# Two decoder layers on one core: key norms in four token quarters, three main passes behind each small product, pooling's products one gate strip later

## The chip, the core and the metric

The kernel runs on one core of a Trainium2 chip. TensorE multiplies, VectorE (DVE) and ScalarE (ACT) do the elementwise work, GpSimd (POOL) a little of it, and the queues of SyncE (SP) and ScalarE issue transfers. The metric is the device time of one execution in microseconds (us), lower is better.

## What is computed

Two layers are applied to 288 tokens: 256 of a prompt and 8 groups of 4 sample tokens. Each layer is a SwiGLU feed-forward block, a mixer, and a second feed-forward block. The mixer adds an RWKV-7 recurrence and a causal pooling, each behind a sigmoid gate. What matters here, cut from the reference:

```python
kk = hs((k * k_k).astype(f32))                       # 8 heads of 64
kk = kk / jnp.maximum(jnp.sqrt(jnp.sum(kk * kk, axis=-1, keepdims=True)), 1e-12)
k = hs(k.astype(f32) * (1 + (a - 1) * k_a.astype(f32)))
S_T, y = lax.scan(_wkv_step, wkv0, (r, decay, k, v, -kk, kk * a))   # over the tokens
d = pooled - pb                                      # windows of 2, 4, 8, 16 tokens
y = jnp.einsum('blgc,gcd->blgd', d, w_pool)
merged = gates[..., :D_MODEL] * (ya @ w_br_a) + gates[..., D_MODEL:] * (yb @ w_br_b)
x = x + mod[:, :, 5] * (merged @ w_out)
```

`kk` is the removal key: it is divided by its norm over each head, for each token.

## The kernel before, in words

Activations lie with features on the 128 partitions and the 288 tokens along the free axis. Weights arrive in slots of eight 128x128 tiles (`raw`, three buffers). Every four tiles ScalarE writes the rounded part `wh` (L225) and VectorE the remainder `wl` (L226); `mm3` then makes three matmuls of each tile (L251), chained in one fixed order. These are the main passes.

The mixer has two streams for TensorE. The first are its main passes, yielded by `main_ops` two tiles at a time, so a step is six main matmuls. There are 136 steps in a layer: 22 strips of four steps (`MAIN`: the input projections "in" 5 to 14; gates "ga" 8 and 9; pooling's four input strips "in" 15 to 18, each followed by one of the gate strips 10 to 13; gate strips 14 and 15), eight strips "bb" of two steps, and eight gate strips 0 to 7 of four steps. After them come the strips "ba", which read the recurrence's result, and then "wo".

The second stream is the recurrence: small fp32 products with ScalarE and VectorE work between them. Its order in the code is: `lora_mm` and the squared keys; norms (`kps`, `rn`) and running decay sums; scaled keys `AR` and `BK`, for which `head_spread` copies a row per head onto 64 partitions; four `scores`; a triangular elimination on VectorE (L945, L947); products that invert blocks; then a loop over four chunks of 64 tokens with state `S`; `outputs(0)` and `outputs(1)` with a group norm; transposes, and `split` into `yah` and `yal`, which "ba" reads. Beside it run the sample tokens' products: `smp_state` four times, and `smp_last` four times, each of which loads a 256 KB state into one shared buffer and writes it back.

The two streams are merged by hand. `fill()` takes its next count from `PLAN` and pops that many items of a queue; with an empty queue an item is one main step. `add` puts a small product on the queue, and `WEAVE` main steps behind it. `need(99)` runs all main steps that are left. A planner then orders the instructions of each engine by this order as priority and by its own durations, and may pull main passes forward where it expects TensorE to be free.

Pooling: `pooled(g)` runs on VectorE after strip "in" 15+g and writes `dd` (two buffers); `pool_out(g)` multiplies it (L706) after a gate strip, and writes `ybh`, `ybl`, which "bb" reads.

The norms before: for each pair of heads `j`, four matmuls put the sums of squares of 288 tokens into rows 32j and 32j+1 of `kps`; a square root, a maximum and a reciprocal run over 128 x 288; `head_spread` reads 32 rows for each pair.

Of the kernel before, what the change touches and what calls it, by code (L numbers as in the profile page):

```python
# [20 lines left out]
AF = mybir.ActivationFunctionType  # L21
# [4 lines left out]
P = 128  # L26
D = 1024
KD = 8
# [7 lines left out]
HP = 4  # L36
# [29 lines left out]
TOK = (0, P, NT - P)  # L66
SLOT = 8
PRIO = 75
WEAVE = 2
PLAN = (1, 0, 0, 11, 1, 15, 12, 16, 5, 6, 2, 0, 10, 12, 2, 2, 1, 8, 13, 1, 2, 8, 4, 2, 3, 0, 5, 1, 1, 7)  # L70
FIRST = 3
RMS = {0: 0.25, 1: 0.15, 2: 0.25}
SPREAD = {0: 0.45, 1: 0.4, 2: 0.45}
# [63 lines left out]
for _n, _w in PARAMS:  # L137
# [1 line left out]
    _o += _w  # L139
NPAR = _o  # L140

CONSTS = [("ones", 1), ("eps", 1), ("ident", 128), ("mhalf", 1), ("hs", 32), ("hb", 128),
          ("maskp", 128), ("masks", 64), ("bmask", 8), ("id32", 32), ("id16", 16), ("halves", 2), ("scan", 288),
          ("rc", 64)]
COFF, _o = {}, 0
# [6 lines left out]
def make_consts():  # L152
    c = np.zeros((P, NCST), np.float32)

    def put(name, a):
        o, w = COFF[name]
        c[: a.shape[0], o:o + w] = a.reshape(a.shape[0], w)

    p = np.arange(P)
    put("ident", np.eye(P, dtype=np.float32))  # L160
    put("mhalf", np.full((P, 1), -0.5, np.float32))
    put("ones", np.ones((P, 1), np.float32))
    hs = np.zeros((P, 32), np.float32)
    hb = np.zeros((P, P), np.float32)
    for e in range(2):
        hs[64 * e:64 * e + 64, e] = 1.0
        hb[e::32, 64 * e:64 * e + 64] = 1.0
    put("hs", hs)
    put("hb", hb)
    s, t = p % 64, np.arange(64)  # L170
    put("maskp", np.stack([s[:, None] < t, s[:, None] <= t], 1).astype(np.float32))
    s, t = p % 32, np.arange(32)
    blk = s[:, None] // TS == t // TS
    put("masks", np.stack([blk & (s[:, None] < t), blk & (s[:, None] <= t)], 1).astype(np.float32))
    put("bmask", ((p % 32)[:, None] // TS == np.arange(NB)).astype(np.float32))
    put("id32", ((p % 32)[:, None] == np.arange(32)).astype(np.float32))
    put("id16", ((p % 16)[:, None] == np.arange(16)).astype(np.float32))
    put("halves", (p % 32 // 16)[:, None] == np.arange(2))
    sc = np.ones(NT, np.float32)
    sc[0:TP:CH] = 0.0  # L180
    sc[TP::TS] = 0.0
    put("scan", np.broadcast_to(sc, (P, NT)))
    rc = np.stack([1.0 / np.minimum(w, np.arange(16) + 1) for w in WINDOWS]).astype(np.float32)
    put("rc", np.broadcast_to(rc, (P, 4, 16)))
    put("eps", np.full((P, 1), NORM_EPS, np.float32))
    return c


class Kernel:
# [433 lines left out]
    def mixer(self, l):  # L623
# [13 lines left out]
        def tj(name):  # L637
# [17 lines left out]
        V.tensor_tensor(out=shs, in0=shs, in1=self.par(l, "mu").unsqueeze(2).to_broadcast([P, NPA, NB]), op=ALU.mult)  # L655
        V.tensor_scalar(mu1, self.par(l, "mu"), -1.0, 1.0, op0=ALU.mult, op1=ALU.add)
        rks = tl([P, HP, 32], "rks")
        G.tensor_tensor(out=rks, in0=self.cst("hs").unsqueeze(1).to_broadcast([P, HP, 32]),
                        in1=self.par(l, "r_k").unsqueeze(2).to_broadcast([P, HP, 32]), op=ALU.mult)
        V.tensor_scalar(ka1, self.par(l, "k_a"), -1.0, 1.0, op0=ALU.mult, op1=ALU.add)  # L660
        ident, hs, hb = self.cst("ident"), self.cst("hs"), self.cst("hb")

        def shifted(i, ps, dst):

# [78 lines left out]
        def main_ops():  # L743

            for n, (name, m) in enumerate(MAIN):
                pre = name == "in" and m < PRE_M
                for ps in strip(name, m, xh=self.vh, xl=self.vl, w=NV) if pre else strip(name, m):
                    yield n
                if (name, m) == ("in", PRE_M - 1):
                    self.v_cm.__exit__(None, None, None)  # L750
                with tc.high_priority(offset=PRIO):
                    if pre:
                        project_pre(m, ps)
                    elif name == "in":
                        project(m, ps)
                    else:
                        S.activation(out=t2s[0][:, m - KD, :], in_=ps[:, :NT], func=AF.Sigmoid,
                                     bias=self.par(l, "b_gate", m))
                if name == "in" and m == 14:
                    nc.sync.dma_start(out=self.io["o_shift"][l], in_=sho)  # L760
                if name == "in" and m == 14:
                    t2s.append(tl([P, KD, NT], "t2"))
                if name == "ga":
                    if m - KD - 2 in dds:
                        pool_out(m - KD - 2, dds[m - KD - 2])
                    self.mod_step()
            at_bb = len(MAIN)
            for m in range(KD):
# [47 lines left out]

        def head_spread(rows, j):
            ps = self.ps_wk()
            T.matmul(ps[:, :NT], hb[32 * j:32 * j + 32, :], rows[32 * j:32 * j + 32, :], start=True, stop=True)
            return ps[:, :NT]  # L820

        halves = [slice(0, 64), slice(64, 128)]
# [8 lines left out]
        for j in range(HP):  # L831
            lora_mm(j)
            t = tl([P, NT], "tj", "kk2", bufs=3)
            S.activation(out=t, in_=xk[:, j, :], func=AF.Square, scale=self.par(l, "k_k", j))
            T.matmul(kps[32 * j:32 * j + 32, :NT], hs, t, start=True, stop=True)
            fill()
        rn = tj("rn")
        S.activation(out=rn, in_=kps[:, :NT], func=AF.Sqrt)
        V.tensor_scalar(rn, rn, 1e-12, None, op0=ALU.max)
        for j in range(HP):  # L840
            V.tensor_tensor_scan(out=cs[:, j, :], data0=self.cst("scan"), data1=sig[:, j, :], initial=0.0,
# [649 lines left out]
```

## Time and profile before

| | |
|---|---|
| time, median of 3 runs (range) | 1428.73 us (1427.41 to 1429.08) |
| the profiled execution: time / span | 1431.08 us / 1429.3 us |
| TensorE busy in the span | 1383.5 us (97%) |
| VectorE, ScalarE, GpSimd busy | 960.1, 722.6, 108.4 us |
| granted TensorE clock, mean | 0.993 |

The span goes from the first to the last instruction. A busy TensorE is not TensorE at its peak, since matmuls overlap; an engine that is not the bottleneck may idle at no cost. Mixer of layer 0 runs from about 280 to 478 us of the span, that of layer 1 from about 980 to 1178 us.

### The profile page before, as it was taken

The numbers are of one execution on the slowest core, as the hardware profiler recorded it, in microseconds if no ns is written. First come the engines' busy times: TensorE is split into PE (matmuls) and PEld (weight loads), VectorE is DVE, ScalarE is ACT, GpSimd is POOL, SyncE is SP. The second block draws the span as 40 slices with busy tenths as digits, with TensorE's granted clock in tenths as the row PEclk, the third lists the DMA queues.
The fourth block names the chain that finished last, engine by engine and source line by source line (L and its number), as shares of the span: only waits on it lengthen the run. The fifth ranks groups of instructions, "written<-read, shape, count | busy, mean of one in ns | idle before, by whom it ended". The sixth has DMA issues, their size and how long they took to land.

```text
span 1429.3 us, 28790 instructions
## 1 busy us (share of the span) xinstructions
PE 1383.5 (97%) x11280; PEld 1282.7 (90%) x11280; DVE 960.1 (67%) x2065; ACT 722.6 (51%) x1460; POOL 108.4 (8%) x151
## 2 busy tenths in 40 slices
PE   6999999999999999999999999999999999999997
PEld 5989999988778999899999999998887899999997
DVE  4645556899766895455667555669996778755554
ACT  4544444675424665444455445448653356555532
POOL 0000002000022010000211000120001200100012
PEclk9999999999999999999999999999999999999999
DMA  8878864443325676787667645454342257445452
GB/s 362 319 269 304 298 249 167 153 142 112 113 66 171 243 268 223 269 303 264 245 246 251 253 149 163 163 175 140 113 139 90 93 185 268 160 163 163 164 170 98
DMA packets 72568, 281.84 MB, mean 197 GB/s; under 512 B 9584, under 2 KB 11760, under 8 KB 63088
## 3 DMA queue, kind: packets, MB, share of 16 engines
q1 hardware_dynamic: 66384, 272.24, 54.4%
q10 hardware_dynamic: 6048, 7.77, 1.8%
q8 instruction: 88, 1.44, 0.4%
q14 instruction: 48, 0.39, 0.1%
HBM read 275.74 MB, written 4.23 MB: 196 GB/s over the span
## 4 chain that ended last, share of the span: by engine, by line
PE 83%; DVE 8%; DMA 3%; issue 2%; ACT 2%; POOL 1%; POOLq 0%; DVEq 0%; ACTq 0%; SPq 0%
PE psmm L251 42%; PE pswk L251 31%; PE psmd L315 4%; DVE wl L226 2%; DMA s<-in_wkv 2%; POOL gn L1110 1%; PE pswk L1048 1%; PE pswk L918 1%; DMA raw<-in_wflat 1%; DVE MM L910 1%; PE pswk L1256 0%; ACT wh L225 0%; PE pswk L814 0%; DMA cc<-in_c 0%; PE pswk L1128 0%
## 5 line engine op out<-in xcount | busy, mean ns | idle before, releaser
L226 DVE TENSOR_TENSOR wl<-raw,wh 128x512 fp32r<-128x512 f32 x732 | 513.3, 704 | 331.0 <-ACT wh L225 322.0
L225 ACT CAST wh<-raw 128x512 fp32r<-128x512 f32 x732 | 452.7, 620 | 550.9 <-PE psmm L251 285.5
L251 PE MATMUL psmm<-uh,wl 128*128 128x288 f32 x1072 | 318.4, 297 | 4.3 <-DVE wl L226 4.3
L251 PE MATMUL psmm<-uh,wh 128*128 128x288 f32 x1072 | 319.8, 298 | 2.2 <-ACT uh L506 2.2
L251 PE MATMUL psmm<-ul,wh 128*128 128x288 f32 x1072 | 318.2, 297 | 0.6 <-DVE ul L507 0.3
L251 PEld LDWEIGHTS psmm<-uh,wh 128*128 128x128 f32 x1072 | 202.1, 188 | 11.3 <-issue 5.1
L251 PEld LDWEIGHTS psmm<-uh,wl 128*128 128x128 f32 x1072 | 202.1, 189 | 9.4 <-DVE wl L226 5.7
L251 PEld LDWEIGHTS psmm<-ul,wh 128*128 128x128 f32 x1072 | 202.0, 188 | 3.6 <-issue 1.7
L251 PE MATMUL pswk<-ul,wh 128*128 128x288 f32 x608 | 179.6, 295 | 0.0
L251 PE MATMUL pswk<-uh,wh 128*128 128x288 f32 x608 | 179.5, 295 | 0.0
L251 PE MATMUL pswk<-uh,wl 128*128 128x288 f32 x608 | 179.5, 295 | 0.0
L251 PEld LDWEIGHTS pswk<-uh,wh 128*128 128x128 f32 x608 | 114.7, 189 | 5.4 <-issue 4.2
L251 PEld LDWEIGHTS pswk<-ul,wh 128*128 128x128 f32 x608 | 114.6, 189 | 0.0
L251 PEld LDWEIGHTS pswk<-uh,wl 128*128 128x128 f32 x608 | 114.5, 188 | 0.0
L251 PE MATMUL pswk<-hl,wh 128*128 128x288 f32 x352 | 103.8, 295 | 0.0
L251 PE MATMUL psmm<-hl,wh 128*128 128x288 f32 x352 | 103.8, 295 | 0.0
L251 PE MATMUL psmm<-hh,wl 128*128 128x288 f32 x352 | 103.8, 295 | 0.0
L251 PE MATMUL pswk<-hh,wl 128*128 128x288 f32 x352 | 103.7, 295 | 0.0
L251 PE MATMUL psmm<-hh,wh 128*128 128x288 f32 x352 | 103.7, 295 | 0.0
L251 PE MATMUL pswk<-hh,wh 128*128 128x288 f32 x352 | 103.2, 293 | 0.0
L315 PE MATMUL psmd<-modw,csilu 128*32 128x512 f32 (+2 forms) x832 | 69.7, 475 | 9.1 <-DMA modw<-in_wmod 9.1
L378 POOL TENSOR_TENSOR sq<-x 128x288 f32<-128x288 f32 x28 | 19.8, 708 | 769.9 <-DVE x L533 769.9
(321 smaller groups left out, 2388.9 us busy)
## 6 DMA issues: line engine op xcount, KB each, us to landing
raw<-in_wflat SPq DMA_DIRECT2D x366, 512.0 KB, 3.3
modw<-in_wmod SPq DMA_DIRECT2D x72, 1024.0 KB, 7.0
s<-in_wkv ACTq DMA_DIRECT2D x16, 256.0 KB, 3.3
o_wkvs<-s SPq DMA_DIRECT2D x8, 256.0 KB, 2.8
x<-in_x SPq DMA_DIRECT2D x1, 1152.0 KB, 5.4
o_y<-yo SPq DMA_DIRECT2D x2, 288.0 KB, 2.5
o_y<-yo ACTq DMA_DIRECT2D x2, 288.0 KB, 2.6
o_pool<-po SPq DMA_DIRECT2D x8, 67.5 KB, 3.0
```

What stands on the lines that cost most here:

```text
L225: self.nc.scalar.copy(wh, src)
L226: self.nc.vector.tensor_tensor(out=wl, in0=src, in1=wh.bitcast(F32), op=ALU.subtract)
L251: self.last = self.nc.tensor.matmul(ps, w, x, start=start and n == 0, stop=stop and n == 2)
L315: mm = nc.tensor.matmul(self.mod_ps[32 * q:32 * q + 32, :size], self.csilu[:, k, :], w[:, kk, q, :], start=(k == 0), stop=(k == KD - 1))
L378: nc.gpsimd.tensor_tensor(out=t, in0=x, in1=x, op=ALU.mult)
L910: V.tensor_tensor(out=MM[:, 2 * e + i, :, q].rearrange("p h x t -> p h (x t)"), in0=pss[e].rearrange("p (h y) -> p h y", h=HP), in1=maskp, ...
L918: T.transpose(ps[:n, 128 * hp:128 * hp + 128], src(hp), ident)
L1048: T.matmul(ps[halves[e], :], ARs[halves[e], hp].rearrange("p x t -> p (x t)"), s0[halves[e]].rearrange("p b v -> p (b v)"), start=True, st ...
L1110: G.tensor_tensor(out=var, in0=var, in1=self.cst("mhalf", n).to_broadcast([n, nh]), op=ALU.pow)
```

## The change

The squared keys of each token quarter (72 tokens) are summed into rows of their own: for pair `j`, four accumulating matmuls of 72 columns write rows 32j+2t and 32j+2t+1 for quarter `t`, with four selection matrices in `hs`. Square root, maximum and reciprocal run over 128 x 72. `head_spread` of `rn` makes four matmuls of 72 columns with four selection matrices in `hb`; `head_spread` of `bsum` remains one matmul of 288. The constants grow by 480 columns (240 KB). `WEAVE` goes from 2 to 3, eight entries of `PLAN` grow, and `pool_out(g)` runs after one more gate strip.

```diff
-WEAVE = 2
-PLAN = (1, 0, 0, 11, 1, 15, 12, 16, 5, 6, 2, 0, 10, 12, 2, 2, 1, 8, 13, 1, 2, 8, 4, 2, 3, 0, 5, 1, 1, 7)
+WEAVE = 3
+PLAN = (1, 0, 0, 11, 1, 15, 14, 18, 5, 6, 2, 0, 12, 13, 4, 4, 3, 9, 13, 1, 2, 8, 4, 2, 3, 0, 5, 1, 1, 7)
...
-CONSTS = [("ones", 1), ("eps", 1), ("ident", 128), ("mhalf", 1), ("hs", 32), ("hb", 128),
+CONSTS = [("ones", 1), ("eps", 1), ("ident", 128), ("mhalf", 1), ("hs", 128), ("hb", 512),
...
-    hs = np.zeros((P, 32), np.float32)
-    hb = np.zeros((P, P), np.float32)
-    for e in range(2):
-        hs[64 * e:64 * e + 64, e] = 1.0
-        hb[e::32, 64 * e:64 * e + 64] = 1.0
+    hs = np.zeros((P, 4, 32), np.float32)
+    hb = np.zeros((P, 4, P), np.float32)
+    for t in range(4):
+        for e in range(2):
+            hs[64 * e:64 * e + 64, t, 2 * t + e] = 1.0
+            hb[2 * t + e::32, t, 64 * e:64 * e + 64] = 1.0
...
-        G.tensor_tensor(out=rks, in0=self.cst("hs").unsqueeze(1).to_broadcast([P, HP, 32]),
+        G.tensor_tensor(out=rks, in0=self.cst("hs")[:, 0:32].unsqueeze(1).to_broadcast([P, HP, 32]),
...
-        ident, hs, hb = self.cst("ident"), self.cst("hs"), self.cst("hb")
+        ident = self.cst("ident")
+        hs, hb = [self.cst(n).rearrange("p (t m) -> p t m", t=4) for n in ("hs", "hb")]
...
                 if name == "ga":
-                    if m - KD - 2 in dds:
-                        pool_out(m - KD - 2, dds[m - KD - 2])
+                    if m - KD - 3 in dds:
+                        pool_out(m - KD - 3, dds[m - KD - 3])
...
         def head_spread(rows, j):
             ps = self.ps_wk()
-            T.matmul(ps[:, :NT], hb[32 * j:32 * j + 32, :], rows[32 * j:32 * j + 32, :], start=True, stop=True)
+            r = quarter[j]
+            n = rows.shape[1]
+            for t in range(NT // n):
+                T.matmul(ps[:, n * t:n * t + n], hb[r, t, :], rows[r, :], start=True, stop=True)
             return ps[:, :NT]
...
-            T.matmul(kps[32 * j:32 * j + 32, :NT], hs, t, start=True, stop=True)
+            for i in range(4):
+                T.matmul(kps[32 * j:32 * j + 32, :NT // 4], hs[:, i, :], t[:, NT // 4 * i:NT // 4 * (i + 1)],
+                         start=i == 0, stop=i == 3)
             fill()
-        rn = tj("rn")
-        S.activation(out=rn, in_=kps[:, :NT], func=AF.Sqrt)
+
+        rn = tj("rn")[:, :NT // 4]
+        S.activation(out=rn, in_=kps[:, :NT // 4], func=AF.Sqrt)
         V.tensor_scalar(rn, rn, 1e-12, None, op0=ALU.max)
```

## Rows read from the trace of the kernel before

**Rows 1.** Windows: both mixers, scores, elimination. Stretch, length, busy us, clock, DMA.

```profile
260.00:464.00 204.00, 192.97 (x1751) 166.36 (x1750) 165.55 (x406) 110.32 (x240) 22.43 (x28) 0.98 0.39 125
960.00:1163.00 203.00, 191.08 (x1750) 165.40 (x1750) 166.22 (x406) 110.60 (x240) 22.04 (x28) 0.99 0.39 126
319.40:327.20 7.80, 5.56 (x67) 4.47 (x66) 7.80 (x17) 2.17 (x6) 0.00 (x0) 1.00 0.27 91
327.20:368.00 40.80, 37.28 (x263) 33.91 (x262) 37.56 (x113) 25.75 (x55) 1.27 (x4) 1.00 0.43 134
```

**Rows 2.** TensorE's waits, whole span: total us, times, longest.

```profile
PE psmm L706 <- DVE dd L695: 4.7, 4, 1.4
PE pswk L1048 <- DMA s<-in_wkv: 3.3, 3, 1.9
PE pswk L906 <- DVE AR L888: 3.2, 2, 1.6
```

**Rows 3.** Windows in the chunk loops; the last number but two is the clock.

```profile
406.00:414.00 8.00, 8.00 (x25) 4.95 (x24) 2.49 (x7) 1.88 (x4) 1.02 (x2) 0.57 0.00 0
1088.00:1094.00 6.00, 6.00 (x65) 4.53 (x63) 3.64 (x9) 1.60 (x4) 1.23 (x2) 0.72 0.15 44
1086.00:1088.00 2.00, 0.29 (x2) 0.22 (x4) 1.03 (x6) 0.42 (x1) 0.00 (x0) 1.00 0.04 14
```

**Rows 4.** The chain that ended last: start us, us, what.

```profile
48.77 3.17 PE psmm L251 x24
```

**Rows 5.** VectorE's groups: forms, count, busy us, mean ns, idle before.

```profile
L413 DVE RECIPROCAL rb<-rb 128x144 f32<-128x144 f32 x10 | 9.8, 1020 | 0.6 <-ACT rb L409 0.6
L843 DVE RECIPROCAL rn<-rn 128x288 f32<-128x288 f32 x2 | 3.9, 1943 | 0.0
```

**Rows 6.** TensorE's timeline at the norms: start us, us, instruction.

```profile
284.75 0.67 PE L835 MATMUL pswk<-kk,consts 128*32 128x288 f32 x2
285.35 0.76 PE L814 MATMUL pswk<-xla,lora 64*128 64x288 f32 x4
...
308.94 0.77 PE L819 MATMUL pswk<-rn,consts 32*128 32x288 f32 x8
309.64 0.40 PE L251 MATMUL psmm<-uh,wh 128*128 128x288 f32 x1
```

**Rows 7.** Transfers: size, median us to landing.

```profile
consts<-in_consts ACTq DMA_DIRECT2D x1, 381.5 KB, 5.2
```

**Rows 8.** TensorE's timeline at the end of layer 0's mixer.

```profile
426.87 1.53 PE L1231 MATMUL pswk<-S,AR 128*64 128x128 f32 x16
...
430.51 1.07 PE L1152 MATMUL pswk<-uv,BKTs 64*64 64x512 f32 x4
...
438.83 0.60 PE L1238 MATMUL pswk<-consts,yn 128*128 128x128 f32 x4
...
465.74 0.29 PE L251 MATMUL psmm<-yah,wh 128*128 128x288 f32 x1
```

**Rows 9.** VectorE's timeline there, with idle time before and its releaser.

```profile
437.24 0.68 DVE L1154 TENSOR_TENSOR s<-s,pswk 128x512 f32<-128x512 f32 x1
...
443.13 0.46 DVE L523 TENSOR_TENSOR yal<-xv,yah 128x288 fp32r<-128x288 f32 x1 [1.10 <-ACT yah L522]
445.70 0.69 DVE L1154 TENSOR_TENSOR s<-s,pswk 128x512 f32<-128x512 f32 x1 [2.11 <-DMA s<-in_wkv]
...
448.73 0.81 DVE L523 TENSOR_TENSOR yal<-xv,yah 128x288 fp32r<-128x288 f32 x2
```

**Rows 10.** ScalarE's waits, 380 to 470 us: total, times, longest.

```profile
ACT wh L225 <- DMA o_wkvs<-s: 4.4, 1, 4.4
ACT yah L522 <- DMA o_wkvs<-s: 3.1, 1, 3.1
```

**Rows 11.** TensorE's waits for split weights, 380 to 470 us, then 1080 to 1170 us.

```profile
PE psmm L251 <- DVE wl L226: 1.9, 2, 1.0
...
PE psmm L251 <- DVE wl L226: 2.4, 2, 1.8
```

## The prediction

> **What bounds the kernel now.** I read the busy shares first: TensorE is busy for 97% of the span, so time can come only from its idle time, from a lower clock, or from fewer products. Main passes run at one every 132 ns, 24 in 3.17 us [rows 4], so a step of six is 0.79 us; the change leaves their number alone. Next I cut the span into windows. Outside the mixers nothing is touched. In the two mixers TensorE is idle for 204 - 193.0 = 11.0 and 203 - 191.1 = 11.9 us [rows 1]. That is nearly all that better order can give, with one addition: in the chunk loops the granted clock falls to a mean of 0.57 over 8 us and 0.72 over 6 us [rows 3], that is, it is in part at 1.2 instead of 2.4 GHz. This costs 8 x 0.43 = 3.4 and 6 x 0.28 = 1.7 us.
>
> The waits say where the idle time lies [rows 2]: for the scaled keys before the scores (3.2 us in both layers together), in pooling's products for `dd` (4.7), in the state products for their load (3.3); and at the mixers' ends for split weights, 1.9 and 2.4 us [rows 11]. In the stage of the scores VectorE is busy for 7.80 of 7.80 us while TensorE is for 5.56 [rows 1]: there VectorE ends last. In the elimination VectorE is at 37.6 of 40.8 us, TensorE at 37.3; both are nearly full.
>
> **The change, part by part.** *The norms on VectorE and ScalarE.* The reciprocal takes 1.943 us for 288 columns and 1.020 for 144 [rows 5]: 6.4 ns a column and 0.1 us fixed, so 0.56 for 72, an estimate from these two. VectorE gets 1.4 us back in each layer, in a stretch where it is full, so the keys `AR` are ready that much earlier. Root and maximum shrink too; I count nothing for them.
>
> *Two steps ahead of the scores.* The entry of `PLAN` before the scores goes from 12 to 14, so two steps of the next gate strip (1.6 us) stand before them. The wait there is 1.6 us in each layer. Either the earlier keys or the two steps would nearly fill it, so I take all 3.2 us off. From nothing (VectorE's queue is reordered and the keys come no earlier, and the steps wait for their `wl`) to 3.2.
>
> *Pooling's products later.* Product g now follows after one more input strip and gate strip, 48 main passes or 6.3 us. The longest wait for `dd` is 1.4 us, so all of them go: -4.7, at least half of it, since VectorE has to feed the main passes that come sooner. `dd` has two buffers, and its first is free only after this product; pooling's third group is written one input strip (3.2 us) later, so that should not wait. If it did, split weights would stand behind it on VectorE's queue. "bb" needs the fourth product's result, which now has one gate strip (3.2 us) before it where it had two.
>
> *Weave of three.* Every queued product has three steps behind it. The state products wait for a 256 KB load into a shared buffer; 0.8 us more between them should remove part of 3.3. I take half, -1.6 (bounds 0 and 3.3). The low clock comes after idle time in layer 1 (TensorE was busy 0.29 of 2 us just before) and after a stretch of small products in layer 0 [rows 3]. With more main passes in that stretch I take back 60% of the 5.1 us: -3.1 (0 and 5.1).
>
> *What TensorE gets on top.* A pass of 288 columns takes 0.30 us alone: `kps` starts at 284.75 and the next product at 285.35, two passes to one fp32 matmul. The four spreads of `rn` took only 0.70 us for eight passes, since each uses its own 32 rows and they overlap [rows 6]. Now 32 passes of 72 columns, a quarter of 0.30 each, come in order of pairs, four matmuls in a row on the same 32 rows: 0.70 us if they overlap as before, 2.40 if not at all. I take 1.9, nearer to no overlap: +1.2 a layer, +2.4 in all (0 to +3.4). The Trainium skill, TensorEngine Tiling (Array Packing), Key Properties, says that different tiles of the array can run matmuls in parallel, which the 0.70 us bears out; for neighbours on one tile it promises nothing, and by that alone this term would be +3.4 and the sum 1.0 us higher. In `kps` eight passes of 72 columns replace two of 288, 0.60 us either way; at the 0.0875 us that a spread's pass took it would be 0.70, +0.8 in all at most, and I take nothing.
>
> *Constants.* 240 KB more on a load of 381.5 KB that takes 5.2 us [rows 7], once, early in the first feed-forward block. The mixer that reads them starts 200 us later, so I cost it at nothing. Uncovered it would be 240/381.5 x 5.2 = 3.3 us.
>
> *The end of the mixer.* This is where it may be given back. I counted pops of `PLAN` by hand. Before, 38 steps are left when `outputs(1)` is issued, 30 of them behind the last transposes: 23.7 us of main passes while VectorE and ScalarE make `yah` and `yal`. After, 12 steps are left at `outputs(1)`, and all are popped ahead of those transposes; the four counts around `split` (2, 8, 4, 2) and `need(99)` find nothing. So "ba" waits openly for the splits. In the trace the transposes start 10.4 us after `outputs(1)` ends (428.40 to 438.83) [rows 8]. The remaining steps and three state products (1.07 us each) take 9.5 + 3.2 = 12.7 us, so the group norm is covered. From the transposes to the end of the first `yal` it is 4.8 us, to that of the last 10.7 us [rows 8, 9]. Less the transposes (0.6), TensorE stands idle for 4.2 us before "ba", and then for up to 4.8 more, since only three quarters of the first strip (1.2 us) can run in the 6.0 us until the last `yal`. Part of those 6 us is a 2.11 us wait of VectorE for a state's load [rows 9], and ScalarE stood 3.1 and 4.4 us for a state's write-back, with `yah` and `wh` behind it [rows 10]. Behind these stand `wl` and `wh`, so TensorE waits for them too. I take 5.6 us a layer, 4.2 and a third of the rest. The 4.3 us of waits for split weights seen there today [rows 11] lie in the same stretch and are replaced: 11.2 - 4.3 = +6.9. The bounds are 0 (the planner pulls the transposes ahead) and 18.0 - 4.3 = +13.7.
>
> **The sum:** -3.2 - 4.7 - 1.6 - 3.1 + 2.4 + 6.9 = -3.3 us. The profiled execution took 1431.08 us, 1.8 outside its span; that leads to 1427.8. It was 2.35 above the median of the runs shown, so in their terms 1428.73 - 3.3 = **1425.4 us**.
>
> **The rivals.** *The tail stands open (slower).* With the latencies of today's trace "ba" waits 9.0 us a layer, and the clock falls again while it waits: -3.2 - 4.7 - 1.6 + 2.4 + 13.7 = +6.6, 1435.3 us. For it speaks that every cover behind the transposes is gone, and the state's round trips through one buffer are no shorter than before; against it that VectorE had other main passes' weights in between, which are then done. Without the clock's gain it decides from 5.7 us of idle time a layer: 2 x 5.7 - 4.3 equals 9.5 - 2.4.
>
> *The clock's gain is lost again (no change).* In layer 1 the clock fell after 1.7 us of idle time [rows 3]; an idle tail of 5.6 us is longer. All else as forecast it gives -0.2, 1428.5 us. The skill's page TensorE: Matmul & The Clock Gate, under HAM oscillation, has gaps in TensorE's work bring the low clock back; rows 3 agree.
>
> *The tail is hidden (clearly faster).* If the planner orders the transposes ahead of the last steps, or the splits run as fast as their engines allow, the term of 6.9 goes: -10.2, 1418.5 us. Against it: the last steps stand ahead in the order that is its priority.
>
> **How the numbers follow.** Forecast 0.35, tail open 0.22, clock lost 0.20, tail hidden 0.23. The predicted time is the forecast's. From the bounds the forecast alone may lie between 1419 and 1431. The full range of the cases goes from 1428.73 - 3.2 - 4.7 - 3.3 - 5.1 = 1412.4 to 1435.3 with 1.0 more for the spreads and 0.8 for `kps`, 1437.1; I leave a tenth out below: 1414.5 to 1437. A measurement here can tell about 0.2%, 2.9 us. Faster by more: hidden, and a little over two thirds of the forecast, 0.48. Slower by more: most of the open tail and a little of the others, 0.25. The rest, 0.27, is within.
>
> **What would show it.** Right: the waits for `AR` and `dd` are gone from TensorE's list; the reciprocal takes about 0.56 us; eight passes become 32 in about 1.9 us; the windows of the chunk loops show clock 1.0; and between the last gate strip and "ba" TensorE has one gap of 4 to 6 us a layer. Wrong: no gap there (faster), a gap of 9 us or a second one inside "ba" and "wo" behind VectorE's waits for states (slower), or waits for `wl` in the elimination as long as those removed, which would mean that VectorE was the bound all along.

## The result and the profile after

The changed kernel takes 1447.83 us (median of 4 runs, 1440.4 to 1452.9) against 1428.07 us for the kernel before (median of 4 runs): ratio 1.013, 95% interval 1.0103 to 1.0157. It is slower by some 20 us. I had forecast 1425.4 us and a range that ends at 1437, so both are wrong. The profiled execution is the slowest of the four (1452.9 us, span 1451.1).

I first split the growth of the span, 1451.1 - 1429.3 = 21.8 us. TensorE's idle time is the span less its busy time: 48.5 us now, 45.8 before, so +2.7. What the clock costs I add up over windows of 2 us, each with 2 x (1 - granted clock): 26.8 us now, 9.7 before, so **+17.1**. The rest, +2.0, is busy time that the clock does not explain. Nearly the whole loss is clock, a term that I had with the other sign. Of the 17.1 us, 13.6 lie in the small products behind the elimination and 5.1 at the mixers' ends; the chunk loops lose 3.4 us, where they lost 5.1.

This holds for more than the profiled execution. Each execution has its mean granted clock on record, to a thousandth (1.4 us). Its span times this clock is the span at full clock if nothing else moved, an estimate: 1421 to 1426 us in the four executions of the changed kernel, 1418 to 1423 in the 13 of the kernel before that ran beside the first experiments. What is left, the loss to the clock, is 13 to 26 us against 3 to 7.

Where it fell is seen in the windows (stretch, length, busy us and instructions by engine, clock, DMA), which answer to [rows 1] and [rows 3]:

```profile
260.00:464.00 204.00, 197.01 (x1809) 174.21 (x1807) 160.46 (x398) 110.87 (x238) 18.14 (x26) 0.97 0.39 121
330.00:370.30 40.30, 40.03 (x293) 37.24 (x293) 37.42 (x114) 26.02 (x56) 1.27 (x4) 1.00 0.43 133
370.30:372.50 2.20, 0.22 (x2) 0.00 (x0) 2.20 (x5) 0.77 (x2) 0.00 (x0) 1.00 0.50 169
372.50:388.00 15.50, 15.48 (x224) 13.25 (x226) 5.90 (x15) 7.85 (x14) 1.68 (x3) 0.56 0.25 74
431.00:440.00 9.00, 9.00 (x58) 7.07 (x58) 3.96 (x9) 4.49 (x9) 0.00 (x0) 1.00 0.34 115
1080.00:1094.00 14.00, 14.00 (x189) 12.02 (x181) 5.35 (x14) 6.92 (x13) 1.51 (x3) 0.51 0.25 81
1106.00:1114.00 8.00, 6.15 (x21) 4.42 (x21) 3.57 (x13) 0.62 (x1) 1.23 (x2) 0.59 0.15 41
```

In the first line, the mixer of layer 0, TensorE is busier than before (197.0 of 204 us against 193.0) and the clock is lower. The next three show where: in the elimination (330 to 370.3 us) TensorE is now busy for 40.03 of 40.30 us, where it was 37.28 of 40.80: the gaps are filled. Then it stands still for 2 us while VectorE is busy for the whole of that window. Right after, in the small products that finish the inverse (called the inverse's products below), the clock is at a mean of 0.56 for 15.5 us, that is mostly at 1.2 GHz. Layer 1 shows the same (1080 to 1094). The line before it (431 to 440) is the stretch in the chunk loop, with the products of `sgl`, where the clock was 0.57 before: there it is 1.00 now, as forecast. The last line is the chunk loop of layer 1, where it is not: 0.59 over 8 us.

TensorE's waits over the whole span (total, times, longest) answer to [rows 2] and [rows 11]:

```profile
PE psmm L252 <- DVE yal L524: 4.7, 3, 2.3
PE pswk L1187 <- DVE Tc L1180: 3.8, 2, 2.0
PE psmm L252 <- ACT yah L523: 3.6, 2, 1.8
PE psmm L252 <- DVE gA L1311: 2.7, 2, 1.6
PE pswk L914 <- DVE AR L896: 2.6, 2, 1.3
PE pswk L1160 <- POOL uv L1157: 2.5, 2, 1.3
PE pswk L1056 <- DVE Gs L1032: 2.1, 1, 2.1
PE psmm L252 <- DVE wl L227: 2.0, 2, 1.0
...
PE pswk L1056 <- DMA s<-in_wkv: 1.6, 3, 1.1
```

The waits for `dd` (4.7 us) are gone, those for state loads halved (3.3 to 1.6). Those for split weights are 2.0 in the whole span, where the mixers' ends alone had 4.3. In their place stand one wait for `Tc` in each layer (3.8) and four kinds at the mixer's end: for `yal` and `yah`, for `gA`, VectorE's sums behind "ba", and for `uv`, the input of the sample tokens' last products (13.5 together). `Tc` is the transposed result of the elimination. One state product of layer 1 now waits 2.1 us for `Gs`, which VectorE makes for the sample tokens, so these products (L1056) wait 3.7 us in all, not less than before. The low clock at 1106 to 1114 stands right behind this wait. The wait for `AR` has hardly moved (3.2 to 2.6).

TensorE's timeline (start us, us, instruction, idle before) shows the `Tc` wait and the tail of layer 0, which answers to [rows 8]; the spreads of the norms answer to [rows 6]:

```profile
285.43 0.69 PE L841 MATMUL pswk<-kk,consts 128*32 128x72 f32 x8
...
309.91 2.63 PE L824 MATMUL pswk<-rn,consts 32*128 32x72 f32 x32
312.47 0.40 PE L252 MATMUL psmm<-uh,wh 128*128 128x288 f32 x1
...
372.52 1.25 PE L1187 MATMUL pswk<-Tc,MM 32*32 32x32 f32 x64 [2.01 <-DVE Tc L1180]
...
465.06 1.07 PE L1160 MATMUL pswk<-uv,BKTs 64*64 64x512 f32 x4 [1.27 <-POOL uv L1157]
466.07 0.66 PE L1246 MATMUL pswk<-consts,yn 128*128 128x128 f32 x4
468.55 0.40 PE L252 MATMUL psmm<-yah,wh 128*128 128x288 f32 x1 [1.83 <-ACT yah L523]
470.99 0.61 PE L252 MATMUL psmm<-yal,wh 128*128 128x288 f32 x1 [2.03 <-DVE yal L524]
```

The 32 spreads hold TensorE from 309.91 to 312.47, 2.56 us where eight took 0.70. The eight narrow passes of `kps` show 0.69 us, the two wide ones 0.67. VectorE's groups have the reciprocal at its forecast (0.56) within 0.04 us, against 1.943 in [rows 5]:

```profile
L851 DVE RECIPROCAL rn<-rn 128x72 f32<-128x72 f32 x2 | 1.2, 596 | 0.0
```

But VectorE's waits between 294 and 323 us, none before, are now

```profile
DVE xv L670 <- ACT sho L669: 1.5, 2, 1.3
DVE AR L879 <- ACT ep L852: 0.8, 1, 0.8
```

so against the 1.35 us that the reciprocal gave back stand 2.3 us of waiting for ScalarE.

### The profile page after: what moved, and what is told of

Same layout as the page of the kernel before. It is cut to its first block, busy times and chain, and to the rows that moved or that the text cites. A ratio compares the mean times of both kernels' runs of the same rounds, so it can differ in the third digit from the quotient of the medians.

```text
span 1451.1 us, 28959 instructions
## 1 busy us (share of the span) xinstructions
PE 1402.6 (97%) x11376; PEld 1303.5 (90%) x11376; DVE 957.7 (66%) x2065; ACT 724.3 (50%) x1460; POOL 107.0 (7%) x151
## 4 chain that ended last, share of the span: by engine, by line
PE 89%; DVE 5%; DMA 2%; issue 2%; ACT 1%; POOL 0%; POOLq 0%; DVEq 0%; ACTq 0%
PE psmm L252 46%; PE pswk L252 31%; PE psmd L316 4%; DVE wl L227 1%; DMA s<-in_wkv 1%; PE pswk L926 1%; PE pswk L1056 1%; PE pswk L824 1%; DVE MM L918 0%; PE pswk L1264 0%; DMA cc<-in_c 0%; PE pswk L1212 0%; DVE gA L1311 0%; PE pswk L1003 0%; PE pswk L1239 0%
```

## The experiments

All kernels compute the whole function. The kernel before ran beside each group, at medians of 1427.25 to 1427.98 us. My theory after the traces: the filled gaps of the elimination come back as one wait for `Tc`, this wait drops the clock in the sparse products behind it, and the open tail and the spreads add to that. The rival: the parts cost in themselves (pooling's order, more products in the queue, narrow passes), or VectorE is the bound and nothing can help.

### Each part alone, and the gap before `Tc` filled

`norms_only` takes from the diff the constants, `kps`, `rn` and `head_spread`; `pool_only` takes the two lines that put pooling's products one gate strip later; `weave_only` takes `WEAVE = 3` and the new `PLAN`. `after_gapfill` is the whole change with main passes drawn forward in front of the products of `Tc`, and as many fewer steps later:

```diff
         fill()
+        ahead(85)              # run main steps until 85 are done
         ps = self.ps_wk()
-        for u in range(16):
+        with tc.issue_after(self.last.ins):
+            for u in range(16):
...
```

> Only the norms over 72 columns; weave of two, the old plan and pooling's products where they were. In the changed kernel's trace the spreads of the norms took 2.6 us a layer where they had taken 0.7, and VectorE won 1.4 us at the reciprocal but then waited for strips that TensorE finished later. Theory (the order of the streams is what costs; the norms cost their products): +1.9 us a layer, at most +4 in all, 1429 to 1432 us, clock as before. Rival (the norms carry most of the loss): above 1436 us.

> Only pooling's products one gate strip later. Theory: VectorE, which is full during the elimination, sets when the inverse is ready. The three waits for dd (2.7 us a layer) then come back in one piece as a wait of TensorE for Tc before the block products, of 2 us or more, and the clock falls to 1.2 GHz in the small products behind it: no gain, 1428 to 1438 us, depending on how long the clock stays low. Rival (the waits for dd were simply a cost): 4 to 5 us faster, about 1423 us, no wait for Tc.

> Only the weave of three and the new plan. No gate strips are left behind the last transposes. Theory: the tail stands open, TensorE waits for yah, yal and the gates of the next products for 5 to 6 us a layer and the clock falls there for some us, while waits for dd stay and keep the wait for Tc short: 4 to 10 us slower than before, 1432 to 1438 us. Rival (the loss is all in the elimination and the clock behind it): 1425 to 1430 us with the tail's waits made up by those gone elsewhere.

> The changed kernel with some 13 main passes and pooling's last product (2.2 us) put ahead of the products that wait for Tc; later counts are lowered by as many, so the rest keeps its order. Theory: the wait for Tc of 2.0 us a layer is what lets the clock fall for the following 12 to 15 us; with it filled the clock stays at 2.4 GHz there and 10 to 15 us of the changed kernel's time come back: 1432 to 1438 us. Rival (the clock falls because the stretch behind has few main passes, whatever stands before it): clock 0.5 there as in the changed kernel, 1444 to 1450 us.

| kernel | median us (runs) | ratio to before, interval |
|---|---|---|
| norms_only | 1437.43 (1436.1 to 1443.1) | 1.0073, 1.0049 to 1.0098 |
| pool_only | 1439.16 (1431.1 to 1451.7) | 1.0082, 1.0051 to 1.0114 |
| weave_only | 1438.38 (1437.9 to 1439.3) | 1.0071, 1.0054 to 1.0088 |
| after_gapfill | 1441.34 (1438.9 to 1442.7) | 1.0091, 1.0074 to 1.0108 |

Each part costs 10 to 12 us alone, 33 together where the whole change costs 20, so the costs do not add; for the norms it is far above what I expected, for the other two just above. The three do not cost the same thing. By span times clock the medians are 1427.5 us (`norms_only`), 1425.8 (`weave_only`) and 1416.7 (`pool_only`), with 1421.4 for the kernel before: on this estimate pooling's order gains 4.7 us, and its ten executions lose 10 to 35 us to the clock. In `pool_only` the windows (here of the slowest of its ten runs) show the loss at full size:

```profile
367.90:370.20 2.30, 0.48 (x4) 0.25 (x2) 2.30 (x5) 1.01 (x3) 0.00 (x0) 1.00 0.83 303
370.20:386.00 15.80, 15.79 (x296) 13.84 (x296) 6.06 (x15) 7.83 (x14) 1.51 (x3) 0.57 0.10 36
...
410.00:430.00 20.00, 20.00 (x85) 11.76 (x83) 6.91 (x15) 2.88 (x6) 1.52 (x3) 0.57 0.08 27
```

So pooling's order alone makes the `Tc` wait (1.8 us in each layer) and the low clock behind it, and in that execution a second low stretch in the chunk loop, with no wait ahead of it. `after_gapfill` is 6.5 us faster than the whole change: the `Tc` wait is gone and the low clock there too (layer 0) or down to 1.7 us (layer 1), but 4.9 us of waits for `dd` are back, the longest 2.6, as the passes drawn forward bring the last product of pooling with them. The time lies between what theory and rival expected; tail and spreads were left as in the change.

### Each cause mended in its own part

`pool_gap` is `pool_only` with the same fill, `ahead(83)`: 18 main passes in a row instead of 8 stand between the last product of pooling and the products of `Tc`. `weave_tail` is `weave_only` with the last steps kept for the tail, where the kernel before had them:

```diff
         def step():
-            at[0] = next(main)
+            if done[0] < limit[0]:     # limit: 106
+                done[0] += 1
+                at[0] = next(main)
...
         transposed(1)
+        limit[0] = 999
```

`norms_tout` is `norms_only` with the 32 spreads in another order, the quarters outside and the pairs of rows inside, so that neighbours stand on different groups of 32 rows:

```diff
+        for t in range(4):
+            for j, r in enumerate(quarter):
+                T.matmul(spread[j][:, n * t:n * t + n], hb[r, t, :], rn[r, :], start=True, stop=True)
         for j in range(HP):
-            ps = head_spread(rn, j)
+            ps = spread[j][:, :NT]
```

`after_tail_tout` is the whole change with the last two mendings, `after_tail` with the tail's alone.

> Only the pooling part of the change, with about ten more main passes (some 1.3 us) placed between the end of the elimination and the small products of the inverse that wait for Tc. Theory (a wait of about 2 us in one piece directly in front of sparse small products drops the clock): the wait for Tc falls from 1.8 us to under 0.8 us in each layer, the stretch of low clock at about 370 to 386 us goes or falls from 6.8 us lost to under 2, and the time is 1425 to 1434 us. Rival (the small products behind fewer main passes are too sparse for the clock whatever stands before them): the stretch stays low, and the time stays at 1436 to 1442 us. A second stretch of low clock at about 410 to 430 us has no wait before it in the run with pooling alone; by the first theory it was a consequence of the first and goes too, by the rival it stays.

> Only the wider weave behind the small products of the chunk loop, with the last main passes held back for the tail as in the kernel before. Theory (what the weave costs is the tail left without main passes): the stretch from ba's first product to wo falls from 19.1 us to under 14 us, the waits for yal, yah, uv and gA fall from 14.3 us to under 5 us in all, and the time is 1424 to 1431 us. Rival (the weave costs by itself, as it delays the small products): the time stays above 1434 us.

> Only the norms' part, with the 16 passes that spread each norm row put in another order: the four quarters outside, the pairs of rows inside, so that neighbours stand on different groups of rows and columns. Theory (neighbours on one tile of the array run one after the other, neighbours on different tiles run over each other): 32 spreads take 0.7 to 1.2 us in place of 2.6, and the time falls by 3 to 4 us to 1433 to 1435 us; the rest of what the norms cost (some 6 us) stays. Rival (the number of passes sets it): they stay at 2.3 to 2.6 us, and the time at 1436 to 1439 us.

> The whole change with the last main passes held back for the tail and the spreads in the order of quarters. Nothing is done here about the wait for Tc, save that the planner puts 17 main passes in front of it. Theory (three causes that add: tail some 7 us, spreads some 4 us, clock in the inverse's products some 8 us): 1434 to 1440 us, with the stretch of low clock behind Tc still there if its wait is over 1.5 us. Rival (VectorE sets the pace and a wait taken from one place comes back at another): 1442 us or more.

> The whole change with the last main passes held back for the tail alone; the spreads stay pair by pair. Theory (tail 6 to 8 us a layer, spreads 1.5 us a layer): 1428 to 1434 us, so the tail carries most of what the run with both mendings won. Rival (the order of the spreads carries it): above 1438 us.

| kernel | median us (runs) | ratio to before, interval |
|---|---|---|
| pool_gap | 1422.37 (1419.7 to 1427.0) | 0.9970, 0.9956 to 0.9984 |
| weave_tail | 1424.57 (1423.3 to 1429.7) | 0.9980, 0.9965 to 0.9996 |
| norms_tout | 1431.91 (1430.7 to 1439.4) | 1.0043, 1.0023 to 1.0064 |
| after_tail | 1433.29 (1426.9 to 1439.5) | 1.0039, 1.0020 to 1.0058 |
| after_tail_tout | 1426.97 (1422.0 to 1430.7) | 0.9997, 0.9982 to 1.0013 |

`weave_tail` and `after_tail` came out where the theory had them, `pool_gap`, `norms_tout` and above all `after_tail_tout` faster.

*Pooling.* With about 1.3 us of main passes more in the gap, `pool_only` becomes 16.8 us faster, below the kernel before. The same products of the inverse, and the chunk loop behind them, now run at full clock in both layers. The windows of layer 0:

```profile
369.90:386.00 16.10, 15.98 (x340) 13.27 (x341) 11.32 (x24) 9.27 (x17) 1.78 (x3) 1.00 0.25 85
...
400.00:424.00 24.00, 23.97 (x252) 17.47 (x249) 15.56 (x36) 5.79 (x13) 8.13 (x9) 1.00 0.18 63
```

Compare 370 to 386 in `pool_only`: 296 matmul instructions at 0.57, here 340 at 1.00. By span times clock the two kernels are 1.6 us apart (1416.7 and 1415.1), so nearly all of the 16.8 us is clock, and pooling's later order is no loss in itself.

*Weave.* Holding the last steps back takes 13.8 us off. TensorE's waits between 425 and 485 us, in `weave_only`:

```profile
PE psmm L251 <- DVE yal L523: 2.7, 1, 2.7
PE psmm L251 <- ACT yah L522: 1.8, 1, 1.8
PE pswk L1152 <- POOL uv L1149: 1.3, 1, 1.3
PE psmm L251 <- DVE gA L1303: 1.0, 1, 1.0
```

and in `weave_tail`, the largest:

```profile
PE pswk L1156 <- POOL uv L1153: 1.4, 2, 1.0
```

The tail's gap was the whole cost of the wider weave. With it closed the weave gains 3 us. In the profiled executions of the pair 8.1 us of the gain are idle time and 4.9 clock.

*Norms.* The 32 passes of `norms_tout` take 1.13 us in place of 2.63, the same passes in another order:

```profile
309.27 1.13 PE L888 MATMUL pswk<-rn,consts 32*128 32x72 f32 x32
```

Passes on the same rows ran one after the other, those on different rows ran over each other, so order and not number set the price. This agrees with the Trainium skill, TensorEngine Tiling (Array Packing), Key Properties: different tiles of the array can run matmuls in parallel. But 4 us remained. The trace of `norms_tout` shows a chain across engines. ScalarE's timeline first, then VectorE's:

```profile
356.05 0.34 ACTq L682 DMA_DIRECT2D po<-in_poolh  x1
...
360.21 0.30 ACT L683 COPY px<-po 128x120 f32<-128x120 f32 x1 [2.72 <-DMA po<-in_poolh]
360.41 0.62 ACT L226 CAST wh<-raw 128x512 fp32r<-128x512 f32 x1
```

```profile
361.06 0.69 DVE L227 TENSOR_TENSOR wl<-raw,wh 128x512 fp32r<-128x512 f32 x1 [1.57 <-ACT wh L226]
```

A small load of pooling's history took 4.2 us, ScalarE stood for it, the weight split `wh` stood behind it in ScalarE's queue, `wl` in VectorE's, and the elimination and `dd` behind that: one wait of TensorE for `dd` is now 3.0 us, where the longest was 1.4.

### The wait alone, in the kernel before

`before_tcwait` has nothing of the change. The transpose that makes `Tc` is done six times, with the same result, and the products of `Tc` are held behind the main passes:

```diff
-        V.transpose(Tc..., Gc...)
+        for _ in range(6):
+            V.transpose(Tc..., Gc...)
```

> The kernel before with nothing of the change: the transpose that makes Tc is done six times instead of once (3.5 us more on VectorE, the result the same), and 14 more main passes (1.9 us) stand in front of the products of Tc, so that TensorE should wait some 1.9 us in one piece there, as it does in the changed kernel. Theory (such a wait in front of sparse small products drops the clock for the whole sparse stretch): a stretch of clock 1.2 GHz of 10 us or more at about 370 to 386 us in each layer, and 1437 to 1447 us. Rival (a wait costs its own length, and the clock fell for another reason): 1430 to 1434 us and no low clock behind Tc.

It took 1452.22 us (1444.2 to 1460.0), ratio 1.0172, 1.0125 to 1.0219: as slow as the changed kernel with nothing of the change, and above the 1447 that I had as its upper end. The repeated transposes came some 1.1 us apart, as other work of VectorE ran between them, so the wait became 4.0 us in each layer and not 1.9. TensorE's waits, then the windows behind them:

```profile
PE pswk L1181 <- DVE Tc L1173: 8.0, 2, 4.0
```

```profile
373.60:386.00 12.40, 12.34 (x246) 11.10 (x248) 5.12 (x13) 6.21 (x11) 1.51 (x3) 0.53 0.25 86
...
1078.20:1092.00 13.80, 13.59 (x268) 12.35 (x270) 5.28 (x13) 6.39 (x11) 1.51 (x3) 0.51 0.24 79
```

The waits for `Tc` are 8.0 - 0.5 = 7.5 us longer, but TensorE's idle time over the span grew by only 2.8 (48.6 against 45.8), as others became shorter (that for state loads 0.7 in place of 3.3). The clock's sum grew from 9.7 to 26.6 us, nearly all of the span's 19.5: 6.8 us in each layer's inverse, and 8.5 in layer 1's chunk loop (1118 to 1136), less the 5.1 that the chunk loops lost before. That loop has no wait of 1.2 us or more ahead of its low stretch, so its part is not shown to come from the wait. The edit also takes 14 main passes out of the stretch behind the wait; but `pool_gap` takes out ten, has no long wait, and keeps its clock there. So in the inverse the clock is the price of that wait, as in the change.

### Everything mended together

`after_mended` is the whole change with tail, spreads and fill (`ahead(85)`); `mended_old_norms` the same with the norms of before. Then, as their sum did not come out, four more: `after_pool4` is `after_mended` with pooling's products one strip later still, filled with main passes alone; `norms_po` is `norms_tout` with the history's loads issued ahead into four buffers, `before_po` the kernel before with that, `pool_gap_norms_po` joins `pool_gap` and `norms_po`.

```diff
-                    if m - KD - 3 in dds:
-                        pool_out(m - KD - 3, dds[m - KD - 3])
+                    if m - KD - 4 in dds:
+                        pool_out(m - KD - 4, dds[m - KD - 4])
...
+        ahead(84)
```

```diff
-            po = tl([P, NC9, HIST], "po", bufs=2)
-            nc.scalar.dma_start(out=po[:, 1:, :], in_=self.io["poolh"][l][:, g])
+            po = pos[g]            # 4 buffers, loaded at the start of the input strip
```

> The whole change with three things mended: the last main passes held back for the tail, the spreads in the order of quarters, and some seven more main passes in front of the products that wait for Tc (24 and 6 in place of 17). If the causes add, what is left of low clock behind Tc (some 7 us in two layers) goes, and the time is 1416 to 1422 us, below the kernel before. Rival (VectorE sets the pace in the elimination and the wait comes back elsewhere): 1425 us or more.

> Pooling and weave with both mendings (tail held back, main passes in front of Tc), and the norms as they were before: 288 columns, 8 spreads. If the two parts' gains add (5.4 us and 3.2 us in the runs of each alone), 1417 to 1421 us. Beside the run with the new norms it shows what the norms' part is worth in good company: theory (the reciprocal's 1.34 us a layer ends in waits for ScalarE, the spreads cost 0.3 us): this one is 0 to 3 us faster; rival (the shorter reciprocal pays): this one is 2 to 4 us slower.

> The whole change with the tail mended, the spreads in the order of quarters, and pooling's products one strip later still, so that 24 main passes that want nothing of VectorE stand in front of the products of Tc and the late pooling product comes behind. Theory (the wait of 2.5 us came from a pooling product placed among the fill): the wait for dd there goes, at most 1.5 us for Tc stays, no low clock in the products of the inverse, 1419 to 1426 us. Rival (VectorE sets the end of this stretch, TensorE waits the same 2 us somewhere): 1429 us or more.

> The norms' part with the spreads in the order of quarters, and the loads of the pooling history issued ahead in the same way. Theory (what is left of the norms' cost is the history that lands late, holds ScalarE for 2.7 us, then the weight split queued behind it, VectorE and at last dd): the wait for dd falls from 6.4 us to under 5 us, and the time to 1425 to 1429 us, that of the kernel before with the same loads. Rival (the narrow norms cost in themselves): 1431 us or more.

> The kernel before, with the four loads of the pooling history issued ahead (four buffers instead of two, the load at the start of the strip before): ScalarE no longer waits for them, some 1.4 us in the elimination of a layer. As a control for the next kernel. Theory (before these waits were short enough not to matter): 1425 to 1429 us. Rival: 1424 us or less.

> Pooling's products later with ten more main passes in front of the products of Tc, plus the norms in the order of quarters and the early loads, and the weave as before. Theory (the norms are worth nothing, and pooling with the filled gap is worth 5 us): 1419 to 1425 us. Rival (the gain of the filled gap hangs on one timing and goes when something shifts): 1428 us or more.

| kernel | median us (runs) | ratio to before, interval |
|---|---|---|
| after_mended | 1430.87 (1429.0 to 1436.6) | 1.0017, 0.9998 to 1.0036 |
| mended_old_norms | 1430.73 (1424.9 to 1437.0) | 1.0017, 0.9995 to 1.0039 |
| after_pool4 | **1419.95** (1419.4 to 1420.7) | **0.9930, 0.9906 to 0.9955** |
| norms_po | 1428.71 (1424.3 to 1431.5) | 0.9999, 0.9983 to 1.0015 |
| before_po | 1430.34 (1427.2 to 1442.7) | 1.0020, 0.9996 to 1.0044 |
| pool_gap_norms_po | 1427.57 (1424.2 to 1437.0) | 0.9995, 0.9972 to 1.0017 |

`after_mended` missed its 1416 to 1422, and `mended_old_norms` its 1417 to 1421. The timeline of `after_mended` shows why, layer 0 and then layer 1:

```profile
373.07 0.72 PE L708 MATMUL psmm<-dd,wpl 128*128 128x288 f32 x2 [2.55 <-DVE dd L697]
...
1072.35 0.72 PE L708 MATMUL psmm<-dd,wpl 128*128 128x288 f32 x2 [2.27 <-DVE dd L697]
```

The passes drawn forward brought pooling's last product in front of `Tc`, and its `dd` stands behind the elimination in VectorE's queue: the same wait under another name. The clock did not answer alike. In layer 0 it fell, in layer 1 it stayed (windows):

```profile
376.00:378.00 2.00, 2.00 (x26) 1.87 (x20) 0.61 (x2) 1.47 (x3) 0.53 (x1) 0.50 0.81 256
...
1074.00:1076.00 2.00, 2.00 (x73) 1.79 (x66) 1.90 (x4) 0.94 (x2) 0.53 (x1) 1.00 0.36 92
```

`after_pool4` puts the late product behind the products of `Tc`. What is left is a wait of 1.0 us, and the clock stays up in both layers. Its timeline, then its windows, the last of them the end of layer 0's mixer:

```profile
370.67 1.20 PE L1207 MATMUL pswk<-Tc,MM 32*32 32x32 f32 x64 [1.04 <-DVE Tc L1198]
...
373.00 0.75 PE L708 MATMUL psmm<-dd,wpl 128*128 128x288 f32 x2
```

```profile
370.70:386.00 15.30, 15.16 (x323) 12.85 (x324) 8.51 (x19) 8.76 (x17) 1.51 (x3) 1.00 0.27 81
1063.20:1078.00 14.80, 14.65 (x319) 12.34 (x320) 8.02 (x19) 8.76 (x16) 1.51 (x3) 1.00 0.22 75
...
440.00:462.00 22.00, 22.00 (x169) 22.00 (x168) 15.87 (x27) 12.53 (x25) 4.01 (x3) 1.00 0.56 181
```

So the change's own idea, with its three side effects mended, is 7.8 us faster than the kernel before (1427.75 in that group) and 27.9 faster than the change as it was made. Against the kernel before its profiled span has 9.6 us less idle time (36.2) and 6.4 us less clock loss (3.3); together that is more than the 11.2 us by which the span is shorter, and the traces do not say where the other 4.8 us went. By span times clock it is at 1414.3 us (median), the kernel before at 1421.3. `after_mended`, `mended_old_norms` and `pool_gap_norms_po` are at 1416.0 to 1416.3: they have most of this gain too, and lose it to the clock (8.6 to 12.9 us in the median, against 4.3).

The norms: `norms_po` is level with the kernel before, where `norms_tout` was 4.1 us above it, and its waits for `dd` are 4.1 us in place of 6.4; `before_po`, the control, does not gain. That fits the chain through the history's load. And the norms' part is worth nothing in good company: `mended_old_norms` and `after_mended` differ by 0.14 us, where each ratio is known to about 0.2%, 3 us.

`pool_gap_norms_po` came out between its theory and its rival and did not keep the gain of `pool_gap`. Its profiled execution has no wait for `Tc`, and yet in layer 0 the clock falls in the inverse's products (windows), while in layer 1 it does not:

```profile
370.00:372.00 2.00, 2.00 (x71) 1.83 (x70) 1.92 (x8) 0.60 (x2) 0.60 (x1) 0.92 0.73 229
372.00:385.00 13.00, 13.00 (x217) 11.54 (x217) 3.72 (x7) 6.27 (x11) 0.99 (x3) 0.50 0.15 48
```

**The tally.** Over the profiled executions, a wait of 1.8 to 4.0 us directly in front of the products of `Tc` stood in ten mixers (both layers of the change, `pool_only`, `after_tail`, `after_tail_tout` and `before_tcwait`), and the clock fell in the inverse's products in all ten. With a wait of 1.1 us or less there, and none over 1.5 for `dd` just before, it fell in one of sixteen (before, `pool_gap`, `after_pool4`, `weave_only`, `weave_tail`, `before_po`, `norms_po`, `pool_gap_norms_po`). This is one execution of each kernel, and the clock differs between executions.

The other kernels are less clear. A wait of 2.3 to 2.7 us for `dd`, six main passes ahead of the products of `Tc`, was followed by a loss of 6.8 us in two mixers, 1.7 in two and none in two (`after_gapfill`, `after_mended`, `mended_old_norms`). A wait's length alone did not set the price. Where main passes followed, 2.5 to 3.0 us for `dd` were followed by a loss of 1.7 us, and the inverse's products ran at full clock (three mixers of `norms_only` and `norms_tout`); 1.8 to 2.1 us for `wl` by none in `pool_only` and `pool_gap`, and 2.0 to 2.2 by 1.7 in `norms_po` and `pool_gap_norms_po`; the 2.1 us for `Gs` in the change by 3.4. Directly in front of the products of `Tc` it was 3.4 to 6.8 each time. A wait of `pool_gap` for `wl`, and the window behind it:

```profile
441.88 0.40 PE L251 MATMUL psmm<-uh,wl 128*128 128x288 f32 x1 [2.13 <-DVE wl L226]
```

```profile
442.00:450.00 8.00, 8.00 (x60) 7.84 (x60) 4.36 (x8) 3.26 (x7) 0.72 (x1) 1.00 0.80 235
```

## Why the prediction was wrong

The step that failed is *Pooling's products later*, "so all of them go: -4.7". The waits for `dd` did go. What I did not ask is what TensorE reaches next: VectorE was at 92% in the elimination and ended no sooner (`Tc`'s products begin at 372.5 us against 368.4), so TensorE came to them 2 us too early. I had written down this very sign, waits in the elimination as long as those removed, but looked for it in `wl`, and gave it no price in clock. The wait for `Tc` went from 0.5 to 3.8 us, so 3.3 of the 4.7 us came back as one wait a layer instead of many, at a place where few main passes follow. The gain itself was there to be had: `pool_gap`, with this wait at 0.5 us a layer, is 5.4 us faster than the kernel before.

The term with the wrong sign is *the clock*, -3.1. Its mechanism held in layer 0, where the `sgl` stretch runs at 1.00; in layer 1 the chunk loop lost 3.4 us, twice what it had, behind the wait for `Gs`. And I read [rows 3] as something that only the chunk loops do, and took a clock gain without asking where the change makes new idle time. It measured +17.1. 13.6 of it stand behind `Tc`. `before_tcwait` shows that a wait there, twice as long, is enough for that part, and `pool_gap` that filling it is enough to lose it. The Trainium skill, TensorE: Matmul & The Clock Gate, under HAM oscillation, which I had cited for the tail, has gaps in TensorE's work bring the low clock back; in [rows 3] layer 1 alone had one. Ten of ten mixers agree with it for the inverse, and the fall in `pool_gap_norms_po`, without a wait for `Tc`, shows that a gap is not the only way.

*Two steps ahead of the scores*, -3.2, measured -0.6. The steps did not come ahead: the trace has the first score products start at 323.82 after a wait of 1.30, and the others at 326.25, with the main passes in between. And `AR` came 2.5 us later (322.45 against 319.95), not 1.4 earlier. VectorE had been full there, without a wait; with the shorter reciprocal it waited 2.3 us for ScalarE, and the product behind the spreads started 2.8 us later than before (312.47 against 309.64).

*The spreads*, +1.2 a layer, measured +1.9: passes on one group of rows do not overlap at all, a little over the upper end of my bound (+1.7). *State loads*, -1.6, measured -1.7, but the same products then waited 2.1 us for `Gs`, so nothing was won.

*The end of the mixer* was right in mechanism, a gap in front of "ba" and a second one inside it, behind `yal`. In layer 0 of the change the waits are 1.27 + 1.83 + 2.03 and 1.1 for `gA`, 6.2 us where I said 5.6 (by its own terms, 4.2 and a third of 4.8, it should have been 5.8). What was too small is its price. Holding the steps back is worth 13.8 us (`weave_only` to `weave_tail`) and 14.5 (the change to `after_tail`), twice my +6.9, since the clock falls at the tail as well (3.4 us at 468 to 476 in the change, none there in `weave_tail`). That the clock falls there too was in my rival of the open tail, which I took for the less likely.

In sequence, on medians of different groups: 1447.8, less 14.5 with the tail's steps held back, less 6.3 with the spreads reordered (by span times clock 3.6 of that are not clock), less 7.0 with the gap before `Tc` filled by the second way tried, makes 1420.0; by span times clock nothing of the 7.0 is left (1414.0 and 1414.3), so it is all clock. What stays open is why the clock falls in one layer and not in the other behind like waits (`after_mended`, `after_gapfill`), and why `pool_gap_norms_po` lost it at all. That the load of the history landed late because weights were moving beside it is argued from the trace, not shown.

## What to carry to other kernels

When a wait is taken away, follow the engine to the next thing it needs from the same supplier: if that supplier does not end sooner, the scattered waits gather into one, and one wait in front of sparse small products can cost several times its length through the clock (in the change 6.8 us of clock for 2.0 us of waiting). Fill such a place with work that wants nothing from the late engine, and see that what you draw forward does not bring a late product along. A cover at the end of a stage is spent only once: more main passes behind the products of the loop are fewer behind the last one.

## What the runs showed of the hardware

- A wait of 1.8 to 2.0 us in front of the inverse's products was followed by 7 to 14 us at 1.2 GHz, though TensorE had work throughout; two waits of 4 us there, in the kernel before, by 6.8 us of clock loss each.
- Where main passes followed a wait of that length or more, the loss was none (2.1 us in `pool_gap`), 1.7 us (behind 2.5 to 3.0 us in `norms_only` and `norms_tout`) or 3.4 (behind 2.1 us in the change).
- The low clock also came without such a wait: 20 us at a mean of 0.57 in `pool_only` while TensorE counted as busy throughout, with 85 matmul instructions in that time.
- 32 fp32 passes of 72 columns on groups of 32 rows took 2.63 us in the order of groups and 1.13 us with the groups in turn.
- Fewer columns did not shorten VectorE's path: a reciprocal of 0.60 in place of 1.94 us saved 1.35 us, and VectorE waited 2.3 us for ScalarE where it had not waited.
